# Wide matmuls ahead of narrow ones in column tiles, and the first two up chunks as one run of 512 columns

## The chip, the cores and the metric

The kernel runs on one core of a Trainium2 chip. A core has engines that work side by side, each through its own queue of instructions in order: TensorE (PE: matmuls; PEld: the load of a matmul's stationary operand), VectorE (DVE), ScalarE (ACT), GpSimd (POOL) and SyncE (SP, which here issues the DMAs). The metric is the device time of one execution in microseconds, lower is better; the time before is the median of three runs.

## What is computed

A trunk of four layers over 256 tokens of width 1024. Each layer has a mixer (layers 0 and 3 differential attention, layer 1 a gated recurrence with decay, layer 2 windowed attention with sinks), a feed-forward network of width 4096, layer norms, and a gated addition of a per-layer embedding:

```python
for i in range(DEPTH):
    kind, j = i % N_MIXERS, i // N_MIXERS
    if kind == 0:
        y = diff_attention(h, da_w_in[j], da_lambda[j], da_subln[j], da_w_out[j], rel_bias, i)
    elif kind == 1:
        y = hgrn2(h, hg_w_in[j], hg_gnorm[j], hg_w_out[j], lb_all[i])
    else:
        y = swa_sink_attention(h, sw_w_in[j], sw_sinks[j], sw_w_out[j], rel_bias)
    h = layer_norm(ALPHA * h + y, ln_g[i, 0], ln_b[i, 0])
    u = jnp.square(jax.nn.relu(h @ w_up[i])) @ w_down[i]
    h = layer_norm(ALPHA * h + u, ln_g[i, 1], ln_b[i, 1])
    h = h + jax.nn.sigmoid(h @ w_ple_gate[i]) * (p[i] @ w_ple[i])
```

All of it is float32.

## The kernel before

**Numbers in two parts.** A product of float32 matrices is made of three matmuls in the type fp32r. `split` (L122) cuts each operand into a high part (ACT, L124) and the rest, a low part (DVE, L125): wh and wl for weights, `hT[0]` and `hT[1]` for the transposed activations. The three products are high × high, high × low and low × high (`mm3`, L175).

**Weights.** They come as 209 chunks of 1 MB (128 partitions × 2048), packed on the host in the order in which they are used. `read_w` (L153) issues the load on SP and splits the chunk in two halves; there are three raw buffers and four chunks of split ones, so that loads and splits run ahead of TensorE.

**Two forms of a product.** *Token-major* (`tokmm`, L182): 128 tokens of hT are stationary, up to 512 columns of weights move, and an output has tokens on its partitions. *Column tiles* (`colmm`, L193): 128 columns of weights are stationary and the tokens move, so that the output comes out transposed, as the next product wants it. For one of the eight slices of depth (kt) a column tile takes two matmuls: a wide one, wh against high and low part of all 256 tokens side by side (512 columns), and a narrow one, wl against the high part (256 columns), which adds to the right half of the bank. They alternate, kt by kt. `join` (L202) then adds the two halves of the bank on ACT and DVE. A chunk holds two tiles (`col2`, L211). Column tiles make the queries, keys and gates of the mixers and all later up chunks of the feed-forward network.

**The feed-forward network** (`ffn`, L421) works in 16 chunks j of 256 columns. The first NA chunks (2, 2, 3 and 2 in the four layers) are made token-major (`up_tok`, L448), in runs of 256 columns for one block of 128 tokens, since then block 0 can start before block 1 has left its layer norm: block 0 of these chunks, with the transposes of the norm's block 1 (`to_hT`, L320) in between, and then block 1. Their output is squared after a ReLU (`relu2`, ACT and DVE), transposed on TensorE (L462) and split into uh and ul by `fin`. The others (`up`, L471) are column tiles, one chunk ahead of the down products, which are token-major with 512 columns, 24 matmuls a chunk (`down`, L499).

**What sets the order.** Work is written as generators in a queue. `fill(us)` (L103) takes steps from the queue until the time that they claim is spent, and so places the small steps of attention or a norm between matmuls; a step of `colmm` is one pair and claims 0.35. A scheduler of the tile framework then fixes each engine's order and may move instructions whose inputs it holds to be ready. `behind` (L132) keeps the splits of later weights behind a marked instruction; `relu2` sets such a mark only for runs of 256.

Of the kernel before, what the change touches and what calls it, by code (L numbers as in the profile page):

```python
# [16 lines left out]
P = 128  # L17
D = 1024
S = 256
KT = D // P  # L20
# [14 lines left out]
LS, LV, RV = 3, 2, 1  # L35
# [33 lines left out]
class Trunk:  # L69
# [122 lines left out]

    def colmm(self, bank, hT, w, col, width):  # L193
        mm = self.nc.tensor.matmul
        for kt in range(KT):
            wh, wl = w.sl(kt * width + col, P)
            mm(bank, wh, hT.both[:, kt].rearrange("p a t -> p (a t)"), start=kt == 0, stop=False)  # L197
            mm(bank[:, S:], wl, hT[0][:, kt, :], start=False, stop=kt == KT - 1)  # L198
            yield 0.35


    def join(self, out, bank, rev=False):  # L202
# [218 lines left out]
    def ffn(self, i, last):  # L421
        nc, tc = self.nc, self.tc
        hT = self.hT
        NJ = 16
        with tc.tile_pool(name=f"fp{i}", bufs=4) as fp:
# [3 lines left out]
            us = {}  # L429

            def new_u(j):
                us[j] = [
                    fp.tile([P, 2, S], F32R, name=self.nm(t), tag=t, bufs=TAIL + 2)
                    for t in ("uh", "ul")
                ]

            def relu2(ps, n):
                r = fp.tile([P, 512], F32, name=self.nm("r"), tag="r", bufs=2)[:, :n]
                x = nc.scalar.activation(r, ps, AF.Relu)
                x = nc.vector.tensor_tensor(r, r, r, op=ALU.mult)  # L440
                if n == 256:
                    self.mark("v", x, RV)
                return r


            wa = {}

            def up_tok(j, blk):  # L448
                if blk == 0:
                    wa[j] = self.load_w()  # L450
                    new_u(j)
                ps = self.mm_ps()
                yield from self.tokmm(
                    ps[:, :256], hT, range(KT), blk, wa[j], [256 * k for k in range(KT)],
                    True, True, n=256,
                )
                r = relu2(ps[:, :256], 256)

                def fin():
                    pt = self.mm_ps()  # L460
                    for c in range(2):
                        nc.tensor.transpose(  # L462
                            pt[:, c * P : c * P + P], r[:, c * P : c * P + P], self.ident
                        )
                    sl = slice(blk * P, blk * P + P)
                    pv = pt[:, :256].rearrange("p (k t) -> p k t", k=2)
                    self.split(us[j][0][:, :, sl], us[j][1][:, :, sl], pv)

                fins.append(fin)

# [10 lines left out]

            fins = []
            na = NA[i]
            for j in range(na):
                self.push(up_tok(j, 0))
            self.fill(2.6 * na - 2.3)
            self.to_hT(self.h[1], 1, hT)
            self.fill_all()
            for j in range(na):
                self.push(up_tok(j, 1))  # L490
            self.fill(1.63)
            for f in fins:
                f()
# [12 lines left out]
            for j in range(NJ - TAIL):  # L506
# [8 lines left out]
                w = self.load_w()  # L515
# [8 lines left out]
            ws = {j: self.load_w() for j in range(NJ - TAIL, NJ)}  # L524
# [18 lines left out]
            for blk in range(2):  # L543
# [3 lines left out]
                ps = [self.mm_ps()[:, :n] for _, n in cols]  # L547
# [616 lines left out]
def _cols(w, cols):  # L1164

    return w[:, cols].reshape(KT, P, len(cols)).transpose(1, 0, 2).reshape(P, -1)


def _half(w):

    t = w.reshape(2, 4, P, 512).transpose(0, 2, 1, 3).reshape(2, P, CH)
    return [t[0], t[1]]


def _rows(w):

    t = w.reshape(-1, 2, P, D).transpose(0, 2, 1, 3).reshape(-1, P, CH)
    return [x for x in t]


def _ffn_chunks(up, down, gate, na):
    def upc(j):
        return _cols(up, np.arange(256 * j, 256 * j + 256))

    dn = _rows(down)
    out = [upc(j) for j in range(na)]
    nup = na
    for j in range(16 - TAIL):
        if nup < 16 and nup < max(j + 2, na + 1):
            out.append(upc(nup))  # L1190
            nup += 1
        out.append(dn[j])
    out += [upc(j) for j in range(nup, 16)]
    out += dn[16 - TAIL :]
    return out + _rows(gate)


def pack(inputs, depth=DEPTH):
# [3 lines left out]
    for i in range(depth):  # L1202
# [31 lines left out]
        if i % 3 < 2:  # L1234
            ch += _rows(a["w_ple"][i])
        ch += _ffn_chunks(a["w_up"][i], a["w_down"][i], a["w_ple_gate"][i], NA[i])

    rel = 255 - np.arange(UL)
# [50 lines left out]
```

## Time and profile before

| | us |
|---|---|
| time, median of 3 runs | 1296.69 (1296.45 to 1298.39) |
| the profiled execution | 1296.76 |
| its span in the trace | 1294.8 |
| TensorE busy | 99% of the span |
| DVE busy, ACT busy | 937.3, 692.0 |
| DMA: mean over the span | 185 GB/s |

The page gives for each engine its busy time, then the span in 40 slices, the chain of work that ended last, and groups of instructions by line. A group's row names line, engine, operation, output<-inputs, shape and count; behind the bar stand busy time in us, mean ns of one instruction, and idle time of the engine ahead of them. Matmuls overlap in TensorE's pipeline, so the mean of one is longer than the distance from its start to the start of the next.

### The profile page before, as it was taken

How to read it: one execution, taken by the hardware profiler on the slowest of the kernel's cores; microseconds unless marked ns; L12 is line 12 of the kernel's file. 1: busy time of each engine (PE TensorE's matmuls, PEld its weight loads, DVE VectorE, ACT ScalarE, POOL GpSimd, SP SyncE). 2: the span in 40 equal slices, each digit the busy share in tenths (PEclk: the TensorE clock that was granted, in tenths of full speed). 3: DMA queues.
4: the chain of work that ended last, by engine and by line, in shares of the span. 5: the costliest groups of instructions: out<-in, count | busy, mean ns of one | idle time of the engine just before them, and what ended most of it. 6: DMA issues, size and time to landing. Idle time of an engine off the chain costs nothing.

```text
span 1294.8 us, 18557 instructions
## 1 busy us (share of the span) xinstructions
PE 1287.8 (99%) x7034; PEld 1087.3 (84%) x7034; DVE 937.3 (72%) x1741; ACT 692.0 (53%) x1296; POOL 35.9 (3%) x48
## 2 busy tenths in 40 slices
PE   9999999999999999999999999999999999999998
PEld 6888888888888888888888788888888888888887
DVE  5888766667889877666677796666687877766666
ACT  5885544444754455444537755444447775444443
POOL 0001000000000010000000000000000010000000
PEclk9999999999999999999999999999999999999999
DMA  8745655553733256555547145655538344655540
GB/s 274 289 171 195 230 193 195 184 189 122 267 127 131 77 211 225 185 190 194 195 166 264 66 166 221 202 191 195 195 131 298 131 171 163 234 191 194 195 162 33
DMA packets 43081, 240.09 MB, mean 185 GB/s; under 512 B 4512, under 2 KB 11744, under 8 KB 16496
## 3 DMA queue, kind: packets, MB, share of 16 engines
q1 hardware_dynamic: 42992, 238.91, 52.8%
q8 instruction: 55, 0.90, 0.3%
q14 instruction: 34, 0.28, 0.1%
HBM read 237.79 MB, written 1.10 MB: 184 GB/s over the span
## 4 chain that ended last, share of the span: by engine, by line
PE 99%; DMA 1%; ACT 0%; DVE 0%; SPq 0%; issue 0%
PE mm L197 24%; PE mm L198 12%; PE acc L177 9%; PE acc L178 9%; PE acc L179 9%; PE mm L177 9%; PE mm L179 9%; PE mm L178 9%; PE acc L1029 2%; PE mm L327 1%; PE mm L684 1%; PE acc L648 1%; PE acc L644 1%; DMA qk<-in_xT_dram 0%; PE acc L857 0%; DMA wr<-in_w_dram 0%
## 5 line engine op out<-in xcount | busy, mean ns | idle before, releaser
L125 DVE TENSOR_TENSOR wl<-wr,wh 128x1024 fp32r<-128x1024 f32 (+1 forms) x548 | 513.8, 967 | 158.4 <-ACT wh L124 157.8
L124 ACT ACTIVATE wh<-wr 128x1024 fp32r<-128x1024 f32 (+1 forms) x548 | 445.6, 852 | 219.4 <-PE acc L179 77.4
L197 PE MATMUL mm<-hT,wh 128*128 128x512 f32 x1344 | 481.6, 400 | 0.0
L198 PE MATMUL mm<-hT,wl 128*128 128x256 f32 x1344 | 377.9, 282 | 0.0
L197 PEld LDWEIGHTS mm<-hT,wh 128*128 128x128 f32 x1344 | 252.6, 188 | 60.0 <-issue 1.8
L198 PEld LDWEIGHTS mm<-hT,wl 128*128 128x128 f32 x1344 | 254.3, 189 | 2.9 <-DVE wl L125 0.4
L177 PE MATMUL acc<-wh,uh 128*128 128x512 f32 x512 | 201.0, 393 | 0.4 <-ACT uh L124 0.4
L178 PE MATMUL acc<-wl,uh 128*128 128x512 f32 x512 | 200.0, 391 | 0.0
L179 PE MATMUL acc<-wh,ul 128*128 128x512 f32 x512 | 199.7, 390 | 0.0
L177 PE MATMUL mm<-wh,hT 128*128 128x512 f32 (+1 forms) x536 | 197.1, 368 | 0.9 <-ACT wh L124 0.8
L178 PE MATMUL mm<-wl,hT 128*128 128x512 f32 (+1 forms) x536 | 193.2, 360 | 0.5 <-DVE wl L125 0.5
L179 PE MATMUL mm<-wh,hT 128*128 128x512 f32 (+1 forms) x536 | 192.8, 360 | 0.0
L204 ACT COPY cr<-mm 128x256 f32<-128x256 f32 x168 | 61.0, 363 | 117.0 <-PE mm L198 116.9
L177 PEld LDWEIGHTS mm<-wh,hT 128*128 128x128 f32 x536 | 101.5, 189 | 16.0 <-ACT wh L124 1.8
L177 PEld LDWEIGHTS acc<-wh,uh 128*128 128x128 f32 x512 | 96.1, 188 | 22.2 <-ACT uh L124 1.9
L179 PEld LDWEIGHTS mm<-wh,hT 128*128 128x128 f32 x536 | 101.3, 189 | 15.8 <-issue 1.0
L179 PEld LDWEIGHTS acc<-wh,ul 128*128 128x128 f32 x512 | 96.2, 188 | 21.1 <-DVE ul L125 0.8
L178 PEld LDWEIGHTS mm<-wl,hT 128*128 128x128 f32 x536 | 101.5, 189 | 14.6 <-DVE wl L125 1.2
L178 PEld LDWEIGHTS acc<-wl,uh 128*128 128x128 f32 x512 | 96.2, 188 | 17.9
L124 ACT ACTIVATE uh<-r 128x512 fp32r<-128x512 f32 x55 | 34.7, 631 | 101.5 <-DVE r L478 101.1
L208 DVE TENSOR_TENSOR r<-mm,cr 128x256 f32<-128x256 f32 x110 | 46.4, 421 | 28.3 <-ACT cr L204 23.0
L318 POOL TENSOR_TENSOR rs<-rp,mhalf 128x2 f32<-128x2 f32 (+2 forms) x36 | 33.1, 918 | 1123.1 <-DVE rp L317 1123.1
(167 smaller groups left out, 983.7 us busy)
## 6 DMA issues: line engine op xcount, KB each, us to landing
wr<-in_w_dram SPq DMA_DIRECT2D x207, 1024.0 KB, 4.9
lng<-in_ln_g_dram SPq DMA_DIRECT2D x8, 512.0 KB, 3.9
lnb<-in_ln_b_dram SPq DMA_DIRECT2D x8, 512.0 KB, 4.6
bt<-ud SPq DMA_DIRECT2D x2, 2048.0 KB, 10.4
wr<-in_w_dram SPq DMA_DIRECT2D x8, 256.0 KB, 5.8
bt<-ud SPq DMA_DIRECT2D x1, 1280.0 KB, 13.3
qk<-in_xT_dram SPq DMA_DIRECT2D x4, 256.0 KB, 5.9
h<-in_x_dram SPq DMA_DIRECT2D x2, 512.0 KB, 11.7
```

Source lines behind the costliest of these rows:

```text
L124: self.nc.scalar.activation(hi, src, AF.Copy),
L125: self.nc.vector.tensor_tensor(lo, src, hi.bitcast(F32), op=ALU.subtract),
L177: mm(out, l[0], r[0], start=start, stop=False)
L178: mm(out, l[0], r[1], start=False, stop=False)
L179: mm(out, l[1], r[0], start=False, stop=stop)
L197: mm(bank, wh, hT.both[:, kt].rearrange("p a t -> p (a t)"), start=kt == 0, stop=False)
L198: mm(bank[:, S:], wl, hT[0][:, kt, :], start=False, stop=kt == KT - 1)
L204: self.nc.scalar.copy(x, bank[:, S:])
L208: self.nc.vector.tensor_tensor(*views, op=ALU.add)
L318: nc.gpsimd.tensor_tensor(out, t, self.mhalf[:, :n], op=ALU.pow)
L327: nc.tensor.transpose(pt[:, j * P : j * P + P], src[:, c : c + P], self.ident)
L1029: nc.tensor.matmul(pl[lo:hi, o : o + w], KS[:, a, b * P + lo : b * P + hi], Qr[:, a, n0 : n0 + g, 1, :], start=True, stop=True,)
```

## The change

Three edits. In `colmm` a column tile issues its eight wide matmuls first and then its eight narrow ones; a step of the generator is now one matmul and claims 0.23 or 0.12. In `ffn` chunks 0 and 1 are made as one token-major run of 512 columns: `up_tok` takes a tuple of chunks, and of its two weight chunks the first now holds the slices 0 to 3 of the depth for all 512 columns and the second the slices 4 to 7 (`_half` in the packing); in layer 2 chunk 2 stays a run of 256. `relu2` sets its mark for both widths.

```diff
     def colmm(self, bank, hT, w, col, width):
         mm = self.nc.tensor.matmul
-        for kt in range(KT):
-            wh, wl = w.sl(kt * width + col, P)
+        ws = [w.sl(kt * width + col, P) for kt in range(KT)]
+        for kt, (wh, _) in enumerate(ws):
             mm(bank, wh, hT.both[:, kt].rearrange("p a t -> p (a t)"), start=kt == 0, stop=False)
+            yield 0.23
+        for kt, (_, wl) in enumerate(ws):
             mm(bank[:, S:], wl, hT[0][:, kt, :], start=False, stop=kt == KT - 1)
-            yield 0.35
+            yield 0.12
...
-                if n == 256:
-                    self.mark("v", x, RV)
+                self.mark("v", x, RV)
...
-            def up_tok(j, blk):
+            def up_tok(js, blk):
+                n = 256 * len(js)
                 if blk == 0:
-                    wa[j] = self.load_w()
-                    new_u(j)
+                    wa[js] = [self.load_w() for _ in js]
+                    for j in js:
+                        new_u(j)
                 ps = self.mm_ps()
-                yield from self.tokmm(
-                    ps[:, :256], hT, range(KT), blk, wa[j], [256 * k for k in range(KT)],
-                    True, True, n=256,
-                )
-                r = relu2(ps[:, :256], 256)
+                kn = KT // len(js)
+                for c, w in enumerate(wa[js]):
+                    yield from self.tokmm(
+                        ps[:, :n], hT, range(kn * c, kn * c + kn), blk, w,
+                        [n * k for k in range(kn)], c == 0, c == len(js) - 1, n=n,
+                    )
+                r = relu2(ps[:, :n], n)
 
                 def fin():
-                    pt = self.mm_ps()
-                    for c in range(2):
-                        nc.tensor.transpose(
-                            pt[:, c * P : c * P + P], r[:, c * P : c * P + P], self.ident
-                        )
...
+                    for i, j in enumerate(js):
+                        pt = self.mm_ps()
+                        for c in range(2):
+                            o = (2 * i + c) * P
+                            nc.tensor.transpose(
+                                pt[:, c * P : c * P + P], r[:, o : o + P], self.ident
+                            )
...
-            for j in range(na):
-                self.push(up_tok(j, 0))
+            groups = [(0, 1), (2,)][: na - 1]
+            for js in groups:
+                self.push(up_tok(js, 0))
...
-    out = [upc(j) for j in range(na)]
+    out = _half(up[:, :512]) + [upc(j) for j in range(2, na)]
```

The order of TensorE in a regular up chunk of layer 0 (mm is the tile's bank in PSUM, x4 four such matmuls in a row). Before, the first half of the first tile:

```order
L197 MATMUL mm_1722<-hT_1284,wh_1714 128x512
L198 MATMUL mm_1722<-hT_1284,wl_1715 128x256
L197 MATMUL mm_1722<-hT_1284,wh_1714 128x512
L198 MATMUL mm_1722<-hT_1284,wl_1715 128x256
L197 MATMUL mm_1722<-hT_1284,wh_1714 128x512
L198 MATMUL mm_1722<-hT_1284,wl_1715 128x256
```

and now the whole chunk, two tiles:

```order
L197 MATMUL mm_1666<-hT_1284,wh_1658 128x512 x4
L197 MATMUL mm_1666<-hT_1284,wh_1662 128x512 x4
L200 MATMUL mm_1666<-hT_1284,wl_1659 128x256 x4
L200 MATMUL mm_1666<-hT_1284,wl_1663 128x256 x4
L197 MATMUL mm_1686<-hT_1284,wh_1658 128x512 x4
L197 MATMUL mm_1686<-hT_1284,wh_1662 128x512 x4
L200 MATMUL mm_1686<-hT_1284,wl_1659 128x256 x4
L200 MATMUL mm_1686<-hT_1284,wl_1663 128x256 x4
```

Both halves of wh (1658 and 1662) are now read before the first half of wl.

The order of DVE in layer 2, where the feed-forward network begins (h_614 and h_615, now h_607 and h_608, are the two blocks of tokens; L338 and L339, now L340 and L341, are the start of a norm, L346 and L351, now L348 and L353, its end; hT is what the transposes leave). Before, from the last splits of the second up chunk to those of the third:

```order
L125 TENSOR_TENSOR wl_7501<-wr_7494,wh_7500 128x1024
L338 SCALAR_TENSOR_TENSOR h_615<-h_615,mm_7288 128x512
L339 BN_STATS bs_7433<-h_615 128x6
L125 TENSOR_TENSOR hT_7367<-mm_7413,hT_7367 128x4x128
L125 TENSOR_TENSOR hT_7367<-mm_7420,hT_7367 128x4x128
L338 SCALAR_TENSOR_TENSOR h_615<-h_615,mm_7289 128x512
...
L351 SCALAR_TENSOR_TENSOR h_615<-h_615,rs_7440,lnb_7364 128x512 x2
L440 TENSOR_TENSOR r_7491<-r_7491 128x256
L125 TENSOR_TENSOR wl_7537<-wr_7534,wh_7536 128x1024
L440 TENSOR_TENSOR r_7531<-r_7531 128x256
L125 TENSOR_TENSOR wl_7541<-wr_7534,wh_7540 128x1024
```

and now:

```order
L125 TENSOR_TENSOR wl_7359<-wr_7352,wh_7358 128x1024
L125 TENSOR_TENSOR wl_7397<-wr_7394,wh_7396 128x1024
L340 SCALAR_TENSOR_TENSOR h_608<-h_608,mm_7176 128x512
L125 TENSOR_TENSOR hT_7255<-mm_7301,hT_7255 128x4x128
L125 TENSOR_TENSOR hT_7255<-mm_7308,hT_7255 128x4x128
L341 BN_STATS bs_7321<-h_608 128x6
L340 SCALAR_TENSOR_TENSOR h_608<-h_608,mm_7177 128x512
L125 TENSOR_TENSOR wl_7401<-wr_7394,wh_7400 128x1024
...
L353 SCALAR_TENSOR_TENSOR h_608<-h_608,rs_7328,lnb_7252 128x512 x2
L442 TENSOR_TENSOR r_7391<-r_7391 128x512
```

The splits of the third chunk (wl_7537 and wl_7541, now wl_7397 and wl_7401) have moved ahead of the norm's end.

A little later in layer 2, behind the transposes of the second block's up results, DVE makes ul for the first down products, from a bank mm that the transposes fill. Before:

```order
L440 TENSOR_TENSOR r_7656<-r_7656 128x256
L208 TENSOR_TENSOR r_7691<-mm_7702,cr_7734 128x256
L440 TENSOR_TENSOR r_7684<-r_7684 128x256
L125 TENSOR_TENSOR ul_7465<-mm_7719,uh_7464 128x2x128
L125 TENSOR_TENSOR ul_7505<-mm_7724,uh_7504 128x2x128
L125 TENSOR_TENSOR wl_7765<-wr_7762,wh_7764 128x1024
```

and now:

```order
L442 TENSOR_TENSOR r_7488<-r_7488 128x512
L442 TENSOR_TENSOR r_7516<-r_7516 128x256
L125 TENSOR_TENSOR wl_7597<-wr_7594,wh_7596 128x1024
L125 TENSOR_TENSOR wl_7601<-wr_7594,wh_7600 128x1024
L125 TENSOR_TENSOR wl_7631<-wr_7628,wh_7630 128x1024
L125 TENSOR_TENSOR ul_7363<-mm_7550,uh_7362 128x2x128
```

Three splits of weights now stand between the last square and ul, where there were none.

More of the change, by code (lines that the diff above doesn't have):

```diff
@@ L440, in relu2 @@
                 x = nc.vector.tensor_tensor(r, r, r, op=ALU.mult)
-                if n == 256:
-                    self.mark("v", x, RV)
+                self.mark("v", x, RV)
                 return r
             wa = {}
-            def up_tok(j, blk):
+            def up_tok(js, blk):
+                n = 256 * len(js)
                 if blk == 0:
-                    wa[j] = self.load_w()
-                    new_u(j)
+                    wa[js] = [self.load_w() for _ in js]
+                    for j in js:
+                        new_u(j)
                 ps = self.mm_ps()
-                yield from self.tokmm(
-                    ps[:, :256], hT, range(KT), blk, wa[j], [256 * k for k in range(KT)],
-                    True, True, n=256,
-                )
-                r = relu2(ps[:, :256], 256)
-                def fin():
-                    pt = self.mm_ps()
-                    for c in range(2):
-                        nc.tensor.transpose(
-                            pt[:, c * P : c * P + P], r[:, c * P : c * P + P], self.ident
-                        )
-                    sl = slice(blk * P, blk * P + P)
-                    pv = pt[:, :256].rearrange("p (k t) -> p k t", k=2)
-                    self.split(us[j][0][:, :, sl], us[j][1][:, :, sl], pv)
+                kn = KT // len(js)
[5 more added lines that the diff above has]
+                r = relu2(ps[:, :n], n)
+                def fin():
+                    for i, j in enumerate(js):
[5 more added lines that the diff above has]
+                            )
+                        sl = slice(blk * P, blk * P + P)
+                        pv = pt[:, :256].rearrange("p (k t) -> p k t", k=2)
+                        self.split(us[j][0][:, :, sl], us[j][1][:, :, sl], pv)
                 fins.append(fin)
@@ L488, in ffn @@
             self.fill_all()
-            for j in range(na):
-                self.push(up_tok(j, 1))
+            for js in groups:
+                self.push(up_tok(js, 1))
             self.fill(1.63)
```

## The prediction

> **What bounds the kernel now.** I read the page first (engines, clock, chain, groups), then the waits, then TensorE's timeline, because an engine that is busy 99% of the span hides its losses between the starts of its instructions.
>
> ```profile
> PE 1287.8 (99%) x7034; PEld 1087.3 (84%) x7034; DVE 937.3 (72%) x1741; ACT 692.0 (53%) x1296; POOL 35.9 (3%) x48
> PEclk9999999999999999999999999999999999999999
> PE 99%; DMA 1%; ACT 0%; DVE 0%; SPq 0%; issue 0%
> L197 PE MATMUL mm<-hT,wh 128*128 128x512 f32 x1344 | 481.6, 400 | 0.0
> L198 PE MATMUL mm<-hT,wl 128*128 128x256 f32 x1344 | 377.9, 282 | 0.0
> ```
>
> TensorE is the chain, at full granted clock. L197 and L198 are the alternating pair of the change, 1344 of each. The durations (400 and 282 ns) overlap in the pipeline, so they price nothing; what counts is the step from one start to the next. The waits of TensorE on other engines are almost nothing, 2.9 us in all:
>
> ```profile
> PE acc L264 <- DVE z L261: 1.2, 1, 1.2
> PE mm L177 <- ACT wh L124: 0.8, 1, 0.8
> PE mm L178 <- DVE wl L125: 0.5, 2, 0.2
> PE acc L177 <- ACT uh L124: 0.4, 1, 0.4
> ```
>
> So there is no wait to remove. A gain must come from shorter steps, and any wait that the new order brings is paid in full. The steps, in TensorE's timeline (start us, duration us; the duration is not used). First one up chunk of two column tiles, from the last wide matmul before it to the first one behind it:
>
> ```profile
> 163.61 0.39 PE L179 MATMUL acc<-wh,ul 128*128 128x512 f32 x1
> 163.84 0.39 PE L197 MATMUL mm<-hT,wh 128*128 128x512 f32 x1
> 164.06 0.28 PE L198 MATMUL mm<-hT,wl 128*128 128x256 f32 x1
> 164.18 0.40 PE L197 MATMUL mm<-hT,wh 128*128 128x512 f32 x1
> ...
> 169.37 0.28 PE L198 MATMUL mm<-hT,wl 128*128 128x256 f32 x1
> 169.48 0.40 PE L177 MATMUL acc<-wh,uh 128*128 128x512 f32 x1
> ```
>
> 163.84 to 169.48 is 5.64 us for 16 pairs, 0.3525 us a pair. Then the steps of matmuls of one width in a row. The 24 wide matmuls of a down chunk, and the narrow (256 columns) token-major ones:
>
> ```profile
> 158.37 0.40 PE L177 MATMUL acc<-wh,uh 128*128 128x512 f32 x1
> ...
> 159.76 0.39 PE L177 MATMUL acc<-wh,uh 128*128 128x512 f32 x1
> ```
>
> ```profile
> 131.93 0.28 PE L178 MATMUL mm<-wl,hT 128*128 128x256 f32 x1
> ...
> 135.65 0.28 PE L179 MATMUL mm<-wh,hT 128*128 128x256 f32 x1
> ```
>
> From 159.76 to 163.84 are 18 steps: 0.2267 us for a wide step that has settled. The first six steps behind a narrow matmul (158.37 to 159.76) take 1.39 us in place of 1.36, so coming out of narrow work costs about 0.03 us once. From 131.93 to 135.65 are 31 steps: 0.120 us for a narrow step. A wide and a narrow step add up to 0.3467, 6 ns below the pair of 0.3525. Alternation seems to pay the price of leaving narrow work again and again. That the excess belongs to the alternation and not to these operands is shown by a stretch right after four transposes, where the same pair does run at the sum:
>
> ```profile
> 139.38 0.39 PE L197 MATMUL mm<-hT,wh 128*128 128x512 f32 x1
> ...
> 141.69 0.28 PE L198 MATMUL mm<-hT,wl 128*128 128x256 f32 x1
> 141.81 0.39 PE L177 MATMUL acc<-wh,uh 128*128 128x512 f32 x1
> ```
>
> Seven pairs from 139.38 to 141.81 take 2.43 us, 0.347 each. The alternating pair thus has two paces, and in the regular part of the feed-forward network it is in the slow one.
>
> **The change part by part.** The sum is made against the profiled execution, 1296.76 us (span 1294.8), 0.07 above the median of the runs.
>
> *Column tiles.* The first tile of a chunk follows wide work: 8 × 0.2267 + 8 × 0.120 = 2.77 us. The second follows narrow work: 0.03 more, 2.80. A chunk takes 5.57 in place of 5.64: 0.07 us less. The feed-forward layers have 55 up chunks in columns (14, 14, 13, 14): 55 × 0.07 = 3.85 us. The attention layers have 29 more chunks (8, 8, 5, 8). There runs are cut by transposes and small matmuls, after which the fast pace is common, and a tile with its entry cost would then be no better than 8 × 0.347; between 0 and 29 × 0.07 = 2.0 I take 0.5, nearer to the row at 0.347. Loads of weights stay as many as before; they are among the steps measured.
>
> *Weights.* All eight wide matmuls now want their high halves within 1.8 us instead of 2.8, while the low halves, which DVE makes last, are wanted later. TensorE waited on weights for 1.3 us in all, so this is free once the first chunks are in; if that cover were gone, at most the 0.8 us of the one wait on wh would be paid again.
>
> *Up chunks 0 and 1 as one run of 512.* Per layer and block 48 narrow steps become 24 wide ones, over 4 layers and 2 blocks 384 × 0.120 = 46.1 us against 192 × 0.2267 = 43.5: 2.55 us less. Of the 480 narrow token-major matmuls (the row and its two sisters at L178 and L179, 160 each) 96 are left.
>
> ```profile
> L177 PE MATMUL mm<-wh,hT 128*128 128x256 f32 x160 | 45.9, 287 | 0.0
> ```
>
> ReLU and square now come once for 512 columns instead of twice for 256. They lie beside matmuls: in layers 0, 1 and 3 the transposes that read the result stand behind nine wide matmuls (2.0 us) of the next block, and behind eight wide and seven narrow ones (2.6 us) at the second place. I cost them at nothing. If that cover is gone, because an engine is inside a weight split when the run ends (1.22 us on DVE, in the rows below), only the part over the cover shows, at eight places.
>
> *DVE's order in layer 2.* Here the order of DVE shows a loss. Both splits of the third chunk (wl_7397, wl_7401) now stand ahead of parts of the norm of the second token block; before, they stood behind it.
>
> ```profile
> 770.80 1.41 DVE L351 SCALAR_TENSOR_TENSOR h<-h,rs,lnb 128x512 f32<-128x512 f32 x2
> 772.46 1.22 DVE L125 TENSOR_TENSOR wl<-wr,wh 128x1024 fp32r<-128x1024 f32 x1
> 773.00 0.28 PE L177 MATMUL mm<-wh,hT 128*128 128x256 f32 x1
> 773.12 0.71 PE L327 MATMUL mm<-ident,h 128*128 128x128 f32 x5
> 790.68 0.73 PE L177 MATMUL acc<-wh,uh 128*128 128x512 f32 x2 [0.35 <-ACT uh L124]
> ```
>
> The norm's last step ended at 772.21; two splits of 1.22 move it to 774.65, its first half to 773.95. TensorE comes to the transposes L327 six narrow matmuls behind the third chunk's first one: 773.00 less 24 × (0.240 − 0.2267) plus 6 × 0.12, so 773.40. It waits 0.55 us, and 0.1 more for the second half. The same layer's first down matmuls wait for uh as before (0.35), but now also for ul, which stands behind three splits of 1.22 on DVE: another 0.4 or so. Queued behind each of these waits is all of TensorE's work. I take 1.0 us, between nothing (DVE has run ahead by then) and 2.0 (both waits in full).
>
> *The rest.* SP issues the same loads in nearly the same order, POOL the same work. TensorE's order has 137 stretches of small matmuls instead of 132, since some transposes are split; a switch already costs the same on each side, so nothing.
>
> Sum: −3.85 − 0.5 − 2.55 + 1.0 = −5.9 us: **1290.8 us**, 0.46% less. A measurement of this kernel tells about 0.2% (2.6 us) from no change.
>
> **Rivals.**
>
> *The order of widths does not matter (1295.2).* If each matmul's step is set by its own width alone, a pair costs 0.3525 in any order, and grouping gives nothing; merging still gives 2.55 and layer 2 takes 1.0: 1296.76 − 1.55 = 1295.2. For it: 0.3525 is only 6 ns above the sum. Against it: 0.347 for the same operands at 139.38, and 0.2267 and 0.120 in long runs. It decides if a tile of eight and eight stays at 2.82. The Trainium skill, "TensorE: Matmul & The Clock Gate", section "Back-to-back issue gap", gives such a rule: a step of the columns over 2.4 GHz plus 2.5 ns whatever stands beside it. That would be 216 and 109 ns, a pair of 325, where the trace has 347 to 353; and merging would give 192 × 2 ns, an estimate of 0.4 us. No stretch quoted here runs at that pace, so the trace bears the rule out only in that width leads. By the page the time would be 1297.4 with layer 2's loss.
>
> *Shorter cover in the attention layers (1301.6, slower).* The planner's fill(x) takes steps until x is spent. The pair counted 0.35; now 0.23 and 0.12 count apart, so a fill stops earlier. fill(2.93) was nine pairs (3.17 us), now eight wide, eight narrow, one wide (3.03); fill(2.6) was eight pairs (2.82), now eight wide and six narrow (2.55). That is 0.41 us less cover per head in 16 heads of differential attention, 6.6 us. By the same count 0.35 in each of eight steps of the windowed attention (2.8) and 0.05 in each of 28 decay levels (1.4): 10.8 us if TensorE gets there before ACT and DVE everywhere, 1290.8 + 10.8. For it:
>
> ```profile
> 366.00:411.00 45.00, 45.00 (x335) 40.13 (x334) 40.52 (x106) 20.90 (x51) 1.49 (x1) 1.00 0.26 88
> 692.00:728.00 36.00, 36.00 (x224) 29.71 (x223) 25.89 (x85) 25.98 (x70) 0.00 (x0) 1.00 0.66 241
> ```
>
> In the decay stage (366 to 411, columns: PE, PEld, DVE, ACT) DVE is busy 40.5 of 45 us. Against it: the windowed stage leaves DVE 10 of 36 us free, the waits above show that TensorE never came early, and the work taken from a fill is done behind the step, not lost. It passes 1296.8 when over half of the 10.8 shows (5.9).
>
> *The entry cost goes too (1287).* If wide runs of eight settle at once and the attention chunks gain as the others: 55 × 0.10 + 29 × 0.07 + 2.55 = 10.1 without layer 2's loss.
>
> That the change does not do what it says is ruled out by the order: most tiles stand as eight and eight, and a few are cut by transposes or by the next tile's wide matmuls.
>
> **How the numbers follow.** Forecast 0.70, rival of equal order 0.14, slower rival 0.10, full gain 0.06. The range reaches from the full gain, 1286.7, past the equal-order rival to 1296.5; outside lie the slower rival and the outermost of the others. Forecast and full gain are faster by over 0.2% (below 1294.1): 0.76. Equal order is within 0.2%: 0.14. Slower by over 0.2%: 0.10.
>
> **What would show it.** Right: in a regular up chunk 5.56 to 5.58 us from its first wide matmul to the next down matmul; inside, wide steps near 0.23 and narrow ones at 0.120; the token-major run at 0.227; a new wait of TensorE in layer 2 near the transposes of the second block. Wrong: narrow steps above 0.124 in the column tiles, which would eat the gain (8 × 0.0044 is the 0.035 that a tile gains); waits of TensorE on softmax or decay tiles beyond those four rows; or a token-major run that waits for its second chunk.

## The result, and the profile after

The changed kernel takes 1290.12 us (median of six runs, 1289.98 to 1291.17); the kernel before took 1297.01 beside it (six runs, 1296.45 to 1298.39). The ratio is 0.9948, with a 95% interval of 0.9937 to 0.9959: 6.9 us less, where 5.9 were forecast. The profiled execution of the changed kernel is its longest, 1291.17 (span 1289.4). In its trace the first column tile starts at 21.41 us, in that of the kernel before at 20.06 (the last section comes back to this), so stages are compared from the first column tile on.

The page and the waits of TensorE after the change:

```profile
PE 1281.5 (99%) x6842; PEld 1078.4 (84%) x6842; DVE 927.2 (72%) x1733; ACT 687.1 (53%) x1288; POOL 34.0 (3%) x48
PE 94%; DVE 3%; ACT 1%; DMA 1%; issue 0%; POOL 0%; SPq 0%; POOLq 0%
L197 PE MATMUL mm<-hT,wh 128*128 128x512 f32 x1344 | 345.3, 395 | 0.1
L200 PE MATMUL mm<-hT,wl 128*128 128x256 f32 x1344 | 190.6, 283 | 0.1
```

```profile
PE mm L177 <- ACT wh L124: 1.2, 2, 0.8
PE acc L266 <- DVE z L263: 1.2, 1, 1.2
PE mm L693 <- ACT prh L124: 0.5, 2, 0.3
PE mm L178 <- DVE wl L125: 0.4, 2, 0.2
PE mm L693 <- DVE e L682: 0.2, 1, 0.2
```

TensorE still bounds the kernel, but it is no longer the whole chain: DVE and ACT hold 4% of it, and two new rows name L693, the transposes of the softmax in differential attention. Waits on softmax tiles beyond the four rows of before were one of the prediction's signs of being wrong; the loss that they belong to is taken up below.

TensorE's timeline of a regular up chunk (start us, duration us; a row with x8 is eight instructions, and the next row's start says when they were done):

```profile
166.75 1.98 PE L197 MATMUL mm<-hT,wh 128*128 128x512 f32 x8
168.56 1.12 PE L200 MATMUL mm<-hT,wl 128*128 128x256 f32 x8
169.51 2.00 PE L197 MATMUL mm<-hT,wh 128*128 128x512 f32 x8
171.35 1.12 PE L200 MATMUL mm<-hT,wl 128*128 128x256 f32 x8
172.31 0.40 PE L177 MATMUL acc<-wh,uh 128*128 128x512 f32 x1
```

166.75 to 172.31 is 5.56 us, and the 43 feed-forward chunks of this form take 5.559 in the mean, in place of 5.640. The first eight wide steps, behind wide work, take 1.81 us, the second eight, behind narrow work, 1.84: the 0.03 of entry cost. And the merged token-major run of layer 0, block 0:

```profile
126.57 0.39 PE L177 MATMUL mm<-wh,hT 128*128 128x512 f32 x1
...
129.97 1.03 PE L329 MATMUL mm<-ident,h 128*128 128x128 f32 x8
```

Its 15 steps take 3.40 us, 0.2267 each.

Where the 6.9 us came from is read from the starts of TensorE's instructions at the borders of the stages (a border is the first transpose of a layer's first or second norm, so that from layer 1 on a mixer's stage also holds the gated embedding of the layer before it):

| stage | before | after | difference |
|---|---|---|---|
| mixer of layer 0, from its first column tile | 97.84 | 100.12 | +2.28 |
| mixer of layer 1 (recurrence) | 176.43 | 175.15 | -1.28 |
| mixer of layer 2 (windowed) | 104.95 | 104.75 | -0.20 |
| mixer of layer 3 | 135.28 | 135.58 | +0.30 |
| feed-forward, layers 0, 1, 3 | 548.61 | 543.16 | -5.45 |
| feed-forward, layer 2 | 181.63 | 179.18 | -2.44 |

The sum is -6.8. The feed-forward layers won 7.9, more than forecast, and the mixers lost 1.1 where 0.5 of gain was forecast.

### The profile page after: what moved, and what is told of

It reads as the page before. It is cut to its first block, busy times and chain, and to the rows that moved or that the text cites. A ratio compares the mean times of both kernels' runs of the same rounds, so it can differ in the third digit from the quotient of the medians.

```text
span 1289.4 us, 18101 instructions
## 1 busy us (share of the span) xinstructions
PE 1281.5 (99%) x6842; PEld 1078.4 (84%) x6842; DVE 927.2 (72%) x1733; ACT 687.1 (53%) x1288; POOL 34.0 (3%) x48
## 4 chain that ended last, share of the span: by engine, by line
PE 94%; DVE 3%; ACT 1%; DMA 1%; issue 0%; POOL 0%; SPq 0%; POOLq 0%
PE mm L197 22%; PE mm L200 11%; PE acc L177 9%; PE acc L178 9%; PE acc L179 9%; PE mm L179 8%; PE mm L178 8%; PE mm L177 8%; PE acc L1038 2%; PE mm L329 2%; DVE wl L125 1%; DMA wr<-in_w_dram 1%; ACT e L670 1%; DVE e L662 1%; PE acc L866 0%
## 5 line engine op out<-in xcount | busy, mean ns | idle before, releaser
L124 ACT ACTIVATE wh<-wr 128x1024 fp32r<-128x1024 f32 (+1 forms) x548 | 438.7, 850 | 194.4 <-PE acc L179 95.3
L197 PE MATMUL mm<-hT,wh 128*128 128x512 f32 x1344 | 345.3, 395 | 0.1
L197 PEld LDWEIGHTS mm<-hT,wh 128*128 128x128 f32 x1344 | 243.7, 188 | 48.7 <-issue 3.2
L200 PEld LDWEIGHTS mm<-hT,wl 128*128 128x128 f32 x1344 | 183.8, 190 | 13.4 <-DVE wl L125 0.3
L200 PE MATMUL mm<-hT,wl 128*128 128x256 f32 x1344 | 190.6, 283 | 0.1
L177 PE MATMUL mm<-wh,hT 128*128 128x512 f32 (+1 forms) x472 | 185.4, 393 | 1.2 <-ACT wh L124 1.2
L178 PE MATMUL mm<-wl,hT 128*128 128x512 f32 (+1 forms) x472 | 182.4, 386 | 0.4 <-DVE wl L125 0.4
L179 PE MATMUL mm<-wh,hT 128*128 128x512 f32 (+1 forms) x472 | 182.5, 387 | 0.0
L177 PEld LDWEIGHTS mm<-wh,hT 128*128 128x128 f32 x472 | 89.2, 189 | 18.3 <-ACT wh L124 2.4
L179 PEld LDWEIGHTS mm<-wh,hT 128*128 128x128 f32 x472 | 89.2, 189 | 18.1 <-issue 1.0
L178 PEld LDWEIGHTS mm<-wl,hT 128*128 128x128 f32 x472 | 89.4, 189 | 16.7 <-DVE wl L125 1.1
L125 DVE TENSOR_TENSOR ul<-r,uh 128x512 fp32r<-128x512 f32 x55 | 38.1, 692 | 34.7 <-ACT uh L124 34.3
```

Source lines behind the costliest of these rows:

```text
L124: self.nc.scalar.activation(hi, src, AF.Copy),
L125: self.nc.vector.tensor_tensor(lo, src, hi.bitcast(F32), op=ALU.subtract),
L177: mm(out, l[0], r[0], start=start, stop=False)
L178: mm(out, l[0], r[1], start=False, stop=False)
L179: mm(out, l[1], r[0], start=False, stop=stop)
```

## The experiments

The theory: TensorE pays when it leaves narrow work, so grouping and merging win in the feed-forward layers; what the mixers lost comes from the planner. Rivals: width alone counts; the gains hang on the order of DVE or ACT; the mixers lost by the grouped order itself.

**The two edits apart.** `e1_group_only` has the grouped `colmm` with the up chunks 0 and 1 as before, `e2_merge_only` the reverse.

> The column tiles grouped, the first up chunks left as two runs of 256 columns each. Theory A (steps: a tile costs 8 x 0.2267 + 8 x 0.120, and 0.03 once behind narrow work; merging is worth 0.0133 us for each of 192 wide matmuls): 2.5 to 3 us slower than the full change, about 1292.8, and a regular up chunk at 5.56 us as in the full change. Theory of equal order (a pair costs 0.3525 whatever the order, so that the gain is the merging's): about 1297, as the kernel before.

> The first two up chunks merged into one run of 512 columns, column tiles alternating as before. Theory A: 2.55 us from the steps, with no loss in layer 2: 1294.4 where the kernel before has 1297.0; with the loss that the prediction saw in layer 2 1295.4. Theory of equal order: all of the gain, about 1290.

Measured: grouping alone 1294.04 against 1297.28 (ratio 0.9973, 0.9964 to 0.9983), merging alone 1294.34 (0.9976, 0.9967 to 0.9985). Both win, so width alone is not the rule: by it grouping would have stayed at 1297. Apart the edits win 3.2 and 2.9, together 6.9. Grouping alone stayed 1.2 above the 1292.8 that were expected: without merging, transposes of up results wait for DVE's squares in layers 0 and 1 (0.8 us more than after the change), and a down matmul of layer 2 still waits for uh. Its trace also shows a first attention layer of 100.27 us, 2.4 longer than before. Merging alone leaves that layer at 97.81, wins 0.5 in each of layers 0, 1 and 3, and 1.3 in layer 2, where a loss had been forecast.

**Grouping in the feed-forward layers only**, with the pair and its 0.35 kept in the mixers:

```diff
+        if not group:
+            for kt in range(KT):
...
+                yield 0.35
+            return
...
-                yield from self.col2(hT, done)
+                yield from self.col2(hT, done, True)
```

> The full change, but the column tiles of the mixers alternate as before, with steps that claim 0.35; only the feed-forward tiles are grouped. By the stages of the two traces the first attention layer lost about 2.4 us behind its first 21 us, the recurrence won 1.2, the others 0.2 or nothing. If these are effects of the mixers' own tiles: about 1 us faster than the full change, 1289. If they come from somewhere else (DMA, the start): no change, 1290.

Measured: 1289.14 (1288.46 to 1289.49), ratio 0.9937 (0.9924 to 0.9949), 1.0 less than the change. Its first attention layer takes 97.77 us and its recurrence what it took before. So in the mixers the change cost more than it won.

**Other claims.** `e4_claims` is the change with 0.21 and 0.111 claimed in place of 0.23 and 0.12, so that a fill takes more steps.

> The full change, with claims of 0.21 and 0.111 in place of 0.23 and 0.12, so that a fill takes as much work ahead of a small step as it did with pairs: fill(2.93) 3.2 us (3.17 before, 3.03 in the change), fill(2.6) 2.77 (2.82, 2.55). Theory A (the first attention layer loses 2.4 us because fills stop earlier and TensorE comes before softmax is done): most of these 2.4 us come back, about 1288. Theory B (it loses because eight wide matmuls ask for all high parts at once, or by where runs are cut): 1290, and waits of over 0.35 us at the transposes of e stay.

Measured: 1289.98 (0.9944, 0.993 to 0.9958), as the change. By the time alone that is Theory B, and a wait of 0.8 us on the softmax is left in the first attention layer. By the stages two effects cancel: the first attention layer falls to 98.64, 1.5 of the 2.3 us that it had lost, and the recurrence loses all but 0.18 of its gain. The wait:

```profile
PE mm L693 <- DVE e L682: 1.2, 2, 0.8
```

So the claims matter, and the same claim does not suit both layers.

**How the price depends on the order.** Three kernels built on `e3_ffn_only` change the groups in the feed-forward layers: both tiles together (16 wide, 16 narrow), groups of four, groups of two. `e5_both_tiles`:

```diff
+        for c in range(2):
+            for kt, (wh, _) in enumerate(ws[c]):
+                mm(pss[c], wh, hT.both[:, kt].rearrange("p a t -> p (a t)"), start=kt == 0, stop=False)
+                yield 0.23
+        for c in range(2):
+            for kt, (_, wl) in enumerate(ws[c]):
+                mm(pss[c][:, S:], wl, hT[0][:, kt, :], start=False, stop=kt == KT - 1)
+                yield 0.12
+            done(c, pss[c])
```

> The feed-forward chunk's two column tiles together: 16 wide matmuls, then 16 narrow ones; merged token-major run as in the change; attention and recurrence alternate as before. Theory (only leaving narrow work costs, about 0.03 us once): the second tile's entry goes, so an isolated up chunk takes 16 x 0.2267 + 16 x 0.120 = 5.547 or a little less, 5.54, in place of 5.56; 55 x 0.02 = 1.1 us less than e3_ffn_only, 1288.0. Rival (the gain of grouping is the length of a run alone and is used up at eight): 5.56 and 1289.1. Rival (both tiles now end together, so the split of the first one starts 0.9 us later and the down matmuls come to wait for it): new waits of TensorE at the first down matmul, 1290 or more.

and `e6_fours` (`e7_twos` has 2 in place of 4):

```diff
-        for kt, (wh, _) in enumerate(ws):
+        for g in range(0, KT, 4):
+            for kt in range(g, g + 4):
...
+            for kt in range(g, g + 4):
```

> As e3_ffn_only, but each tile in the feed-forward layers goes four wide, four narrow, four wide, four narrow. A chunk leaves narrow work three times in place of one (15 in the alternating order). If each such turn costs the same, the excess over the sum of the widths is shared out evenly: (5.640 - 5.559) / 14 = 6 ns a turn, so a chunk takes 5.559 + 2 x 6 = 5.57. If a turn behind four or more narrow ones costs what the traces show behind eight (0.014 to 0.03 us), a chunk takes 5.587 to 5.62. If only the lengths count and four are too short, 5.64. Time: 1289.1 plus 55 times the difference of the chunk to 5.559: 1289.8, 1290.7 to 1292.5, 1293.6.

> As e3_ffn_only, but each tile in the feed-forward layers goes in groups of two wide and two narrow. A chunk leaves narrow work seven times. Even price of 6 ns a turn: 5.559 + 6 x 6 ns = 5.595, time 1291.1. Price of 0.014 us or more a turn: 5.64 or more (as the alternating order or worse), time 1293.6 or more. If the gain is there only from a length of eight on: 5.64.

The timeline of one chunk of each, first 16 and 16, then the fours, then the twos:

```profile
207.84 3.79 PE L235 MATMUL mm<-hT,wh 128*128 128x512 f32 x16
211.46 2.08 PE L239 MATMUL mm<-hT,wl 128*128 128x256 f32 x16
213.38 0.40 PE L177 MATMUL acc<-wh,uh 128*128 128x512 f32 x1
```

```profile
207.99 1.07 PE L205 MATMUL mm<-hT,wh 128*128 128x512 f32 x4
208.89 0.64 PE L208 MATMUL mm<-hT,wl 128*128 128x256 f32 x4
209.37 1.09 PE L205 MATMUL mm<-hT,wh 128*128 128x512 f32 x4
210.30 0.63 PE L208 MATMUL mm<-hT,wl 128*128 128x256 f32 x4
...
213.57 0.40 PE L177 MATMUL acc<-wh,uh 128*128 128x512 f32 x1
```

```profile
208.09 0.62 PE L205 MATMUL mm<-hT,wh 128*128 128x512 f32 x2
208.55 0.40 PE L208 MATMUL mm<-hT,wl 128*128 128x256 f32 x2
208.78 0.63 PE L205 MATMUL mm<-hT,wh 128*128 128x512 f32 x2
...
213.66 0.40 PE L177 MATMUL acc<-wh,uh 128*128 128x512 f32 x1
```

Over the 43 chunks the means are 5.539, 5.587 and 5.563 us. Both tiles together are at the 5.54 that was expected, and the time is 1288.34 (1288.22 to 1288.93; ratio 0.9934, 0.9922 to 0.9946), 0.8 below `e3_ffn_only` where 1.1 was expected; no wait appeared at the down matmuls. The fours and the twos were run once each, so the means of their chunks say more than their times. The fours are at 1291.95 and 5.587, the lower end of the second reading (a turn costs about as much as behind eight). The twos fell outside every reading: with seven turns they take less than the fours with three, at 1289.38. The number of turns is therefore not what counts. With the chunk of `e5_both_tiles` as zero, one turn costs 0.020 us in eights, 0.016 in fours, 0.0035 in twos and 0.007 in the alternating order. The steps show why a sum over turns fails: entering wide work the steps are 0.233, 0.236, 0.228, 0.232 and 0.231 before they settle at 0.2267, which adds 0.027, while the first narrow step behind wide work is 0.113 and the second 0.119, which gives 0.008 back. In twos the narrow pairs go at 0.113 + 0.119 or 0.116 + 0.112, so the reward comes back each time while the price is cut off by the next turn. What in TensorE does this, these traces do not say.

**What cost the first attention layer 2.3 us.** `e8_fine_steps` is `e3_ffn_only` with the mixers' pairs in alternating order, but yielding 0.23 and 0.12 one by one:

```diff
                 mm(bank, wh, hT.both[:, kt].rearrange("p a t -> p (a t)"), start=kt == 0, stop=False)
+                yield 0.23
                 mm(bank[:, S:], wl, hT[0][:, kt, :], start=False, stop=kt == KT - 1)
-                yield 0.35
+                yield 0.12
```

> As e3_ffn_only, with the order of widths in attention and recurrence as before (alternating), but the planner is told of the wide and the narrow matmul one by one (0.23 and 0.12) in place of 0.35 for the pair. Theory A (what the change lost in the first attention layer, 2.3 us, and won in the recurrence, 1.2 us, comes from the finer steps in which the fills are dealt out and cut): both come back here, 1289.1 + 2.3 - 1.2 = 1290.2. Theory B (it comes from the grouped order itself): none of it here, 1289.1. Mixed: the recurrence wins without the first attention layer losing, 1287.9, or the reverse, 1291.4.

Measured: 1292.13 (1291.51 to 1292.45), 3.0 more than `e3_ffn_only` and 0.7 over the nearest reading, the loss without the recurrence's gain (1291.4). The first attention layer takes 100.64 us, all of the loss without one grouped tile in it; the recurrence gains 0.1. So the loss comes from the finer steps, and the recurrence's gain needs the grouped order. `e10_fill` asks how the finer steps cost it. It is the changed kernel with the two fills of the head loop raised to what the alternating order really took:

```diff
-                self.fill(2.93)
+                self.fill(3.15)
...
-                self.fill(2.6)
+                self.fill(2.8)
```

> The changed kernel with two arguments of the planner raised to the steps that the alternating order really took, in the head loop of differential attention alone: fill(2.93) to fill(3.15) and fill(2.6) to fill(2.8). Theory (the first attention layer lost 2.3 us because its fills stop earlier, so that softmax and transposes are reached too soon): most of it comes back, 1290.1 - 2.0 = 1288.1, and the first attention layer is near the 77.5 us that the alternating order takes there. Rival (it is the finer cutting of the column runs, or the grouped order itself, that costs): 1290, as the change.

(The 77.5 in that text is a slip: the layer takes 97.8 us in the alternating order; its start at 20 us had been taken off twice.) Measured: 1287.65 (1287.16 to 1287.92; ratio 0.9925, 0.9912 to 0.9937), 2.5 below the change, and a first attention layer of 97.62. Two windows of that layer show the idle time (us; columns behind the length: busy PE, PEld, DVE, ACT, POOL), before, after and with the longer fills:

```profile
20.00:60.00 40.00, 39.98 (x246) 33.16 (x246) 31.36 (x104) 30.02 (x91) 2.09 (x2) 1.00 0.86 318
60.00:98.00 38.00, 38.00 (x222) 30.98 (x221) 32.12 (x106) 29.32 (x90) 3.15 (x4) 1.00 0.51 175
```

```profile
20.00:60.00 40.00, 39.78 (x236) 32.52 (x236) 30.64 (x100) 29.26 (x86) 1.42 (x2) 1.00 0.84 301
60.00:98.00 38.00, 37.41 (x217) 29.90 (x216) 32.57 (x105) 30.13 (x91) 2.31 (x3) 1.00 0.62 218
```

```profile
20.00:60.00 40.00, 39.93 (x246) 32.94 (x245) 31.36 (x104) 29.99 (x91) 2.11 (x2) 1.00 0.87 318
60.00:98.00 38.00, 37.99 (x224) 31.36 (x223) 32.52 (x108) 29.36 (x90) 3.15 (x4) 1.00 0.59 201
```

TensorE idles 0.02 us before, 0.81 after (0.22 + 0.59) and 0.08 with the longer fills. That is a third of the loss. With the rest, the timeline shows more interruptions: small matmuls cut into column and token-major runs 22 times before, 28 times after, 19 times with the longer fills. One of the places after the change:

```profile
69.65 0.39 PE L197 MATMUL mm<-hT,wh 128*128 128x512 f32 x1
70.26 0.33 PE L693 MATMUL mm<-ident,e 128*128 128x128 f32 x1 [0.22 <-DVE e L682]
70.34 0.48 PE L197 MATMUL mm<-hT,wh 128*128 128x512 f32 x1
70.66 0.43 PE L693 MATMUL mm<-ident,e 128*128 128x128 f32 x2
```

A wide step of 0.23 became 0.61 (69.65 to 70.26) in front of a transpose that came too early, and each return to column work costs again (70.34 to 70.66 is 0.32 for one wide matmul). The number of cuts alone does not measure the loss: `e8_fine_steps` loses 2.8 us with 24 of them. How much of the other 1.5 us is cuts and how much is waits that the busy time hides stays open; that the length of the fills brings it all back is shown.

**Layer 2.** `e11_layer2` is `e3_ffn_only` with chunks 0 and 1 of layer 2 apart again:

```diff
-            groups = [(0, 1), (2,)][: na - 1]
+            groups = [(0,), (1,), (2,)] if na == 3 else [(0, 1)]
```

> As e3_ffn_only, with chunks 0 and 1 of layer 2 alone apart again (three runs of 256 columns there, as before). By the prediction's term (merging costs layer 2 a loss of 1.0 us in DVE's order against 0.64 us won in width) this is 0.36 us faster than e3_ffn_only: 1288.8. By the traces of the change and of e2_merge_only (the loss did not come, and merging took away a wait of the kernel before at the first down matmuls) it is 0.8 to 1.2 us slower: 1289.9 to 1290.3, with a wait of about 0.6 us at the first down matmul of layer 2.

Measured: 1290.64 (1289.75 to 1290.84; ratio 0.9946, 0.9932 to 0.996), slower than `e3_ffn_only` by 1.5, of which its trace puts 1.1 in the feed-forward network of layer 2; the other stages agree within 0.05, and its first column tile starts 0.6 later (20.88 and 20.24). A down matmul waits again there:

```profile
787.09 0.39 PE L177 MATMUL acc<-wh,uh 128*128 128x512 f32 x1
787.66 0.50 PE L177 MATMUL acc<-wh,uh 128*128 128x512 f32 x1 [0.18 <-ACT uh L124]
```

0.57 us from the one before it to its start, 0.34 over a step, about half of what was expected. Merging is thus a gain in layer 2, as in the others and larger.

**What won, put together.** `e9_best` is `e5_both_tiles` with grouped tiles in the recurrence and the windowed attention, while differential attention alternates; `e12_all` groups there too, with the fills of `e10_fill`.

> e5_both_tiles with the column tiles of the recurrence and of the windowed attention grouped as in the change (eight wide, eight narrow); the two differential attention layers go on alternating. If the 1.2 us that the change won between the first feed-forward layer and the second, and the 0.2 in the windowed layer, belong to the grouped order there: 1288.3 - 1.4 = 1286.9. If they hung on what stands before them in the program: 1288.3.

> All that won put together: both tiles of a feed-forward chunk as 16 wide and 16 narrow, grouped tiles in all three kinds of mixer, and the two fills of e10_fill. If the parts add up, e10_fill less what e5_both_tiles won over e3_ffn_only (0.8): 1287.65 - 0.8 = 1286.9; that is e9_best less the 0.2 to 0.3 us by which the grouped attention layer with longer fills beat the alternating one in the trace. If the longer fills take work that is missed later, 1287.5 or more.

Measured: 1287.09 (1286.82 to 1287.57; ratio 0.9921, 0.9908 to 0.9935) and 1286.88 (1286.44 to 1287.27; 0.9921, 0.9907 to 0.9935). Both came out as the sum of their parts, and both beat the change by 3 us, about 10 below the kernel before. Between the two there is no difference that these runs can tell.

## Why the prediction was right, and where its terms were not

The time came within 0.7 us of the forecast, and that is partly luck: layer 2 came out better by 1.7 us and the mixers worse by 1.6.

| term | forecast | measured in the trace |
|---|---|---|
| column tiles of the feed-forward layers | -3.85 | -5.0 |
| merging in layers 0, 1, 3 | -1.9 | -1.6 |
| layer 2: merging -0.64, DVE's order +1.0 | +0.4 | -1.3 |
| column tiles and fills of the mixers | -0.5 | +1.1 |

*Column tiles.* The mechanism was right: 5.56 us a chunk inside the forecast window, an entry cost of 0.03 at the second tile, narrow steps at 0.120. The rival of equal order is out. So is the step that the prediction takes from the Trainium skill ("TensorE: Matmul & The Clock Gate", section "Back-to-back issue gap"): wide steps settle at 0.2267 here and not at 0.216. The section gives that formula for a matmul taken alone, which the prediction does not say. What the term left out lies behind the chunk: coming from alternating work, the down matmuls paid an entry too, and now pay less. In layer 0 all steps of down matmuls take 85.45 us in place of 85.62, and those of the column tiles, the cut ones too, 77.93 in place of 79.02: 1.26 for 14 chunks, 0.09 each, times 55 is 5.0. A regular chunk by itself gains 0.081; the sum used the 0.07 that came out of rounded steps.

*Merging.* The steps were as forecast, 0.2267. In each of the three layers 0.51 to 0.55 came in place of 0.64, since the entry into wide work has its price here too, behind transposes. In layer 0 the 96 narrow steps took 11.67 us, 0.15 over 96 × 0.120; the 48 wide ones take 11.12, 0.24 over 48 × 0.2267, nearly all of it in the first steps behind two groups of transposes (0.316, 0.233 and 0.236 behind the second).

*Layer 2.* This step failed. It costed the norm's delay and a second wait at the first down matmuls on top of the wait that was there before. The trace of after, first DVE, then TensorE:

```profile
771.19 1.41 DVE L353 SCALAR_TENSOR_TENSOR h<-h,rs,lnb 128x512 f32<-128x512 f32 x2
```

```profile
771.77 0.28 PE L179 MATMUL mm<-wh,hT 128*128 128x256 f32 x1
772.07 0.63 PE L329 MATMUL mm<-ident,h 128*128 128x128 f32 x4
```

The norm's last step ends at 772.60. The program is 1.50 us ahead of the kernel before at this layer's first norm, so this is 1.9 later in the program than 772.21, not 2.4, and TensorE waited 0.18 at 771.77 (a step of 0.30 in place of 0.12) and not 0.55. The larger part is at the first down matmuls. Before, the one at 790.68 waits for uh, which ACT makes behind a copy and a ReLU. TensorE, then ACT:

```profile
789.50 0.60 PE L462 MATMUL mm<-ident,r 128*128 128x128 f32 x4
789.85 0.48 PE L177 MATMUL acc<-wh,uh 128*128 128x512 f32 x1
```

```profile
789.70 0.37 ACT L204 COPY cr<-mm 128x256 f32<-128x256 f32 x1 [1.71 <-PE mm L198]
789.96 0.39 ACT L439 ACTIVATE r<-mm 128x256 f32<-128x256 f32 x1
790.24 0.67 ACT L124 ACTIVATE uh<-mm 128x256 fp32r<-128x256 f32 x2
```

The step from the down matmul ahead of it took 0.83 us (789.85 to 790.68 in the prediction's row), 0.60 over a settled step. After the change (TensorE, ACT, DVE):

```profile
786.81 0.82 PE L470 MATMUL mm<-ident,r 128*128 128x128 f32 x6
787.58 0.39 PE L177 MATMUL acc<-wh,uh 128*128 128x512 f32 x1
788.04 0.39 PE L179 MATMUL acc<-wh,ul 128*128 128x512 f32 x1
```

```profile
787.22 0.94 ACT L124 ACTIVATE uh<-mm 128x256 fp32r<-128x256 f32 x3 [1.56 <-PE mm L470]
```

```profile
778.07 1.09 DVE L125 TENSOR_TENSOR ul<-mm,uh 128x256 fp32r<-128x256 f32 x3 [1.07 <-ACT uh L124]
785.09 3.49 DVE L125 TENSOR_TENSOR wl<-wr,wh 128x1024 fp32r<-128x1024 f32 x3
788.50 1.08 DVE L125 TENSOR_TENSOR ul<-mm,uh 128x256 fp32r<-128x256 f32 x3
```

No down matmul waits now. The copy and the ReLU no longer stand ahead of uh, which follows 0.41 behind the transposes (786.81 to 787.22), and ul does stand behind three splits, as forecast. But TensorE's own order has changed as well. The first six down matmuls (787.58 to 788.72) are now whole groups of three, with ul among them at 788.04; the ul of the second block comes only at 788.50, so they work on the first block's, made at 778.07, and a column tile follows at 788.97. Before, the down matmuls ahead of the column tile (789.85 to 791.02) all read uh, and the first with ul stands at 794.48. The prediction kept TensorE's order of the down matmuls as it was and looked for what is late on DVE.

*The mixers.* The term was set near nothing from the pace of the pairs; the rival of shorter cover put a price of 10.8 on the fills if all of it showed. Its mechanism is real in differential attention, where the longer fills of `e10_fill` bring the loss back: 2.3 us in the first attention layer and 0.3 in the fourth, against 6.6 at most by its count for both. It did not show in the decay stage or the windowed attention. The recurrence gained 1.3 instead, and not by its pairs: the steps at the transposes of its output (12 among themselves and 3 ahead of them) fell from 2.81 to 2.00 us, most of it at one group (414 us in the trace of before) that had stalled and no longer does, while the column matmuls gained 0.8 inside their runs and gave 0.6 back where the runs are cut. Alternating with fine steps does not do it, and grouping with the smaller claims does not either, so it hangs on both order and claims; which instruction was late there was not tried.

## What to carry to other kernels

Where TensorE is never idle, look at the distance between starts by what stood before: matmuls of two widths can be cheaper in long groups, and the price of changing over is read from rows and not from the number of changes. When such a regrouping also changes the grain of what a planner deals out, check each fill's length again, since a fill that ends one step sooner can cost more than the regrouping wins there, as in the first attention layer here. A wait that the profile already shows is part of the sum: before adding a new wait to it, ask whether the new order keeps the old one, on both feeding engines and on the one that waits.

## What the runs showed that was not expected

Groups of two are better than groups of four (5.563 against 5.587 us a chunk), and taken with the down matmuls behind them better than groups of eight: in layer 0 the column tiles and the down matmuls take 163.30 us in twos, 163.39 in eights (`e3_ffn_only`), 164.04 in fours and 163.15 as 16 and 16. The chunk is 0.004 us longer in twos than in eights, but the down matmuls of the layer take 85.30 in place of 85.46.

In four of fourteen profiled executions, that of the change among them, five to seven wide steps between 7 and 12 us take 0.43 us in place of 0.23. The window of the first 20 us (third number from the end: mean granted clock) and two such steps, in the run of the change:

```profile
0.00:20.00 20.00, 17.15 (x54) 10.32 (x55) 9.48 (x15) 9.96 (x16) 0.74 (x7) 0.91 0.70 219
```

```profile
9.44 0.63 PE L179 MATMUL mm<-wh,hT 128*128 128x512 f32 x1
9.87 0.63 PE L177 MATMUL mm<-wh,hT 128*128 128x512 f32 x1
```

Between 9.4 and 12.0 us the granted clock of this run is 0.51. Six such steps are 1.2 us of TensorE's time, and this run reaches its first column tile 1.35 us later than the kernel before. What such a start costs is not settled, though: `e4_claims` has seven such steps and reaches its first column tile at 20.22, `e3_ffn_only` has none and is there at 20.24. The granted clock does not always tell: `e12_all` has five such steps, and the same window shows 1.00:

```profile
0.00:20.00 20.00, 17.89 (x59) 11.21 (x60) 10.46 (x17) 10.95 (x18) 0.74 (x7) 1.00 0.70 225
```

In the Trainium skill, "TensorE: Matmul & The Clock Gate", section "Back-to-back issue gap", the gap from one matmul to the next, with the array at its lower clock, is the columns over 1.2 GHz. For 512 columns that is an estimate of 0.427 us, and the trace agrees with its 0.43 (9.44 to 9.87).
